# A weight slice loaded in two pieces, and the first four products in another order

## The chip, the cores and the metric

The kernel runs on one core of a Trainium2 chip. The metric is the device time of one execution in microseconds (us). Three executions of the kernel before took 1918.41, 1918.44 and 1919.22 us; the median is 1918.44.

## The reference, cut to what matters

One layer of a decoder trunk is computed for 320 tokens (256 of a prompt, 64 new ones of eight sequences), 2048 channels wide, in float32. All weights are read once.

```python
h = rmsnorm(x, norm_mix_g)
b_a, c_a, v_a, glu_a, glu_b, gate_a, gate_b = split(h @ w_in)        # 2048 -> 7 x 2048
y_a = (b_a * causal_dwconv3(c_a * v_a)) @ w_out_a
u = glu_a * sigmoid(glu_b)
z = silu(layernorm(causal_dwconv31(u) + bias))
y_b = z @ w_out_b
x = x + (sigmoid(gate_a) * y_a + sigmoid(gate_b) * y_b) @ w_o
h2 = rmsnorm(x, norm_ffn_g)
x = x + (silu(h2 @ w_gate) * (h2 @ w_up)) @ w_down                   # 2048 -> 5632 -> 2048
y = rmsnorm(x, final_norm_g)
```

The last rows of both convolutions' inputs are outputs as well.

## The kernel before, in words

**Products.** Every matrix product is made of 128 x 128 blocks of weights against 320 tokens. To keep float32's precision, weights and activations are each split in a high part (rounded to float32r) and a low part (the rest). Each block then needs three matmuls: weight high x activation high (line 268), weight high x activation low (line 270), weight low x activation high (line 272). In the code, `prod` in `begin` issues them, and its argument `which` selects one of the three (0, 1, 2).

**Units and pieces.** A unit is 256 output columns (two blocks j = 0 and 1, each with its own accumulator) over all of the contraction. Its weights come in pieces of four contraction chunks k, 512 KB each. ACT makes the high part and DVE the low part (lines 226 and 230 for whole pieces).

**The opening.** The first three units of `w_in` run as a group (`run_group`), because the activations also have to arrive. In the first round (r = 0, chunks k = 0 to 3) every chunk serves all three units m = 0, 1, 2 in turn. The weights of this round and the chunks of x are packed into few transfers: `op0` (the gains and x's chunk 0, into the tile `lead`), `op1` (chunk 0 of the three units' weights, 256 columns each) and `op2` (for k = 1 to 3: x's chunk and the three weight slices), all of these into the tile `opening`.

**Queues of the opening (lines 97 to 105).** SP issues `lead`; ACT issues the first 128 columns of unit 0's slice (64 KB); SP issues unit 0's second 128 columns with unit 1's 256 columns as one transfer (192 KB, line 99); ACT issues unit 2's slice (128 KB); SP goes on with the four transfers of `op2` (288, 256, 544 and 544 KB, line 104), and then, in `load_x` (line 117) and `load_part` (line 183), with further chunks of x and raw weight pieces. Later transfers are issued as earlier ones land.

**The splits of the opening.** `at_start` calls `x_chunk(k)`: x times its gain, high part (DVE, line 410, for k = 0 and 1; ACT, line 412, after that) and low part (DVE, line 413). Then `open_split(m, k)` for m = 0, 1, 2: high part on ACT (line 1032), low part on DVE (line 1033). For the very first slice the high part is made in two halves of 128 columns, the first from ACT's transfer and the second from SP's; its low part is one instruction over both halves. `in_turn` keeps the order on ACT and DVE.

**What sets the order.** A planner with a modelled time line orders the instructions of each engine, but `tc.issue_after(x)` holds an instruction behind x. In `run_group` the variable `last_mm` chains the matmuls: for k = 0 every product is chained to the one before it, so that they run exactly in the order of `turns`; for later k only every second product (j = 1) moves the chain on, and the planner may order the six matmuls of a pair. In `turns` an entry is (m, j, f): unit, block, and which of the three products (None for all).

Ahead of the first product TensorE runs 12 matmuls on zeros (line 123), which need no load.

Of the kernel before, what the change touches and what calls it, by code (L numbers as in the profile page):

```python
# [15 lines left out]
P = 128  # L16
# [14 lines left out]
NB = 256  # L31
# [8 lines left out]
def trunk_kernel(ctx: ExitStack, tc: tile.TileContext, a):  # L40
# [44 lines left out]
    sp, aq = nc.sync, nc.scalar  # L85
# [6 lines left out]
    opening = io.tile([P, 2 * D], F32, tag="pair", name="opening")  # L92
# [3 lines left out]
        opened[m][0] = opening[:, m * NB : (m + 1) * NB]  # L96
    sp.dma_start(out=lead, in_=a["op0"])
    aq.dma_start(out=opening[:, 0:P], in_=a["op1"][:, 0:P])
    sp.dma_start(out=opening[:, P : 2 * NB], in_=a["op1"][:, P : 2 * NB])
    warmed = aq.dma_start(out=opened[2][0], in_=a["op1"][:, 2 * NB :]).ins  # L100
    for k in range(1, KP):
        o = opening[:, 3 * NB + (k - 1) * W : 3 * NB + k * W]
# [85 lines left out]
    def load_to(i):  # L188
        while nload[0] <= min(i, len(pieces) - 1):
            load_part(nload[0], 0, pieces[nload[0]]["n"], sp)  # L190
            if nload[0] in after_load:
                after_load[nload[0]]()
            nload[0] += 1

    def split_to(i):
        while nsplit[0] <= min(i, len(pieces) - 1):
            q = pieces[nsplit[0]]
            if nsplit[0] > 2:
                load_to(nsplit[0])
            n = q["n"]  # L200
            if "apart" in q:
                q["hi"] = [slot("wh", F32R)[:, :NB] for _ in range(n)]
                q["lo"] = [slot("wl", F32R)[:, :NB] for _ in range(n)]
                for k in range(n):
                    last_split["ac"] = ac.copy(out=q["hi"][k], in_=q["raw"][:, k, :]).ins
                    last_split["ve"] = ve.tensor_tensor(
                        out=q["lo"][k], in0=q["raw"][:, k, :], in1=q["hi"][k].bitcast(F32), op=ALU.subtract
                    ).ins
                nsplit[0] += 1
                continue  # L210
            h = wp.tile([P, KP, NB], F32R, tag="whi", name=nm("whi"))
            l = wp.tile([P, KP, NB], F32R, tag="wlo", name=nm("wlo"))
            q["hi"], q["lo"] = h, l
            if nsplit[0] > 3:
                split(q, 0, n)
            nsplit[0] += 1
# [39 lines left out]
    def begin(u):  # L256
        acc = [ps_acc.tile([P, 512], F32, tag="acc", name=nm("acc")) for _ in range(u["nj"])]
        hi, lo = u["acts"]()
        hi_, lo_ = lambda k: alt(hi[k]), lambda k: alt(lo[k])
        nk = u["nk"]  # L260

        def prod(q, k, j, which=None):
            kk = q["ka"] + k
            wh = q["hi"][:, k, j * P : (j + 1) * P]
            wl = q["lo"][:, k, j * P : (j + 1) * P]
            o = acc[j][:, :T]
            if which in (None, 0):
                last = te.matmul(o, wh, hi_(kk), start=(kk == 0), stop=False)  # L268
            if which in (None, 1):
                last = te.matmul(o, wh, lo_(kk), start=False, stop=False)  # L270
            if which in (None, 2):
                last = te.matmul(o, wl, hi_(kk), start=False, stop=(kk == nk - 1))  # L272
            return last.ins

        return acc, prod
# [3 lines left out]
    def run_group(us, at):  # L279

        on = [begin(u) for u in us]
        for k in range(KP):
            u0 = [pieces[u["pieces"][0]] for u in us]
            if k == 0:
                turns = [(0, j, f) for j in range(2) for f in range(2)]
                turns += [(m, j, f) for f in range(2) for m in (1, 2) for j in range(2)]
                turns += [(m, j, 2) for m in range(3) for j in range(2)]
                for m in range(3):
                    at(0, m, k)
            else:  # L290
                turns = [(m, j, None) for m in range(3) for j in range(2)]
            for m, j, f in turns:
                if k and j == 0:
                    at(0, m, k)
                with tc.issue_after(last_mm[0]):
                    last = on[m][1](u0[m], k, j, f)
                if k == 0 or j:
                    last_mm[0] = last
        for r, m, k in [(r, m, k) for r in range(1, NC // KP) for m in range(3) for k in range(KP)]:
            u = us[m]  # L300
            pi = u["pieces"][r]
            acc, prod = on[m]
            load_to(pi + DMA_AHEAD)
            at(r, m, k)
            if k == 0:
                with tc.issue_after(x_last["ac"]), tc.issue_after(x_last["ve"]):
                    split_to(pi + 1)
            with tc.issue_after(last_mm[0]):
                for j in range(2):
                    last = prod(pieces[pi], k, j)  # L310
            last_mm[0] = last
            if r == NC // KP - 1 and k == KP - 1:
                u["post"](acc)
# [825 lines left out]
    load_to(6)  # L1139
    split_to(2)  # L1140
    run_group(first_units, at_start)
    for what, budget, kw in seq:
        if callable(what):
# [101 lines left out]
```

## Time and profile before

| what | value |
|---|---|
| median of three runs | 1918.44 us |
| the profiled execution's own time | 1918.46 us |
| its span, first to last instruction | 1916.3 us |
| TensorE (PE) busy | 1910.5 us, 14,071 matmuls |
| VectorE (DVE) busy | 1303.9 us |
| ScalarE (ACT) busy | 840.7 us |
| bytes moved by DMA | 321.18 MB |
| first product that belongs to the result | starts at 3.95 us |

How to read the profile: a row of the time line gives the start and the length in us, the engine, the line of the code, the operation, the tile written and the tile read, the shape, the count of merged instructions, and in brackets the idle time of that engine just before and what ended it. PE is the matrix engine and PEld its weight load. SPq and ACTq are issues of transfers by SP and ACT. In lists of transfers the last column is the time from issue to landing. Busy times of PE use modelled ends, so that a start is firmer than an end.

### The profile page before, as it was taken

Reading aid. Unit: us, or ns where it says so; the run is one execution under the profiler, and the core shown is the slowest. Engines: PE = TensorE matmul, PEld = TensorE weight load, DVE = VectorE, ACT = ScalarE, POOL = GpSimd, SP = SyncE. Lnnn points to the kernel's source line nnn. Section 1 sums busy time; section 2 is a strip of 40 time slices with the busy share of each in tenths; the row PEclk is TensorE's granted clock in tenths of the full one; section 3 lists DMA queues with packets and bytes.
Section 4 is the critical chain, followed back from the end, with each engine's and each line's share of the span. In section 5 each row is a group of like instructions: output and inputs, shape, how many; then the busy total and the mean of one; then the engine's idle time right before and its main releaser. Section 6 shows DMA issues by size and latency. Waiting matters only on the chain.

```text
span 1916.3 us, 33970 instructions
## 1 busy us (share of the span) xinstructions
PE 1910.5 (100%) x14071; PEld 1909.6 (100%) x14071; DVE 1303.9 (68%) x1951; ACT 840.7 (44%) x1203; POOL 5.0 (0%) x26
## 2 busy tenths in 40 slices
PE   9999999999999999999999999999999999999998
PEld 9999999999999999999999999999999999999998
DVE  8998888999898788546566655555444555555556
ACT  6544344444444346434445333433333433434543
POOL 0000000000000000000000000000000000000000
PEclk9999999999999999999999999999999999999999
DMA  8565655555555555555565555555555555554554
GB/s 294 177 183 161 196 157 167 161 165 159 165 164 163 159 163 165 159 162 165 164 188 188 163 158 164 164 158 157 160 167 164 165 162 159 164 163 147 176 158 131
DMA packets 96755, 321.18 MB, mean 168 GB/s; under 512 B 12792, under 2 KB 19512, under 8 KB 96568
## 3 DMA queue, kind: packets, MB, share of 16 engines
q1 hardware_dynamic: 96168, 318.61, 53.4%
q8 instruction: 110, 1.80, 0.4%
q10 hardware_dynamic: 432, 0.39, 0.1%
q14 instruction: 45, 0.37, 0.1%
HBM read 315.42 MB, written 4.98 MB: 167 GB/s over the span
## 4 chain that ended last, share of the span: by engine, by line
PE 99%; DMA 0%; DVE 0%; ACT 0%; issue 0%; DVEq 0%
PE acc L270 33%; PE acc L272 33%; PE acc L268 33%; PE acc L825 0%; PE acc L827 0%; PE acc L826 0%; DMA lead<-in_op 0%; PE acc L858 0%; PE acc L850 0%; DVE rl L413 0%; ACT junk L932 0%; DVE rh L410 0%; DVE ye L928 0%; DVE yo L928 0%; DVE rst L928 0%
## 5 line engine op out<-in xcount | busy, mean ns | idle before, releaser
L230 DVE TENSOR_TENSOR wlo<-raw,whi 128x1024 fp32r<-128x1024 f32 (+1 forms) x588 | 709.6, 1207 | 518.5 <-ACT whi L226 515.3
L226 ACT CAST whi<-raw 128x1024 fp32r<-128x1024 f32 (+1 forms) x588 | 607.0, 1033 | 948.5 <-PE acc L270 771.9
L270 PE MATMUL acc<-hl,whi 128*128 128x320 f32 x1600 | 478.1, 299 | 0.0
L272 PE MATMUL acc<-hh,wlo 128*128 128x320 f32 x1600 | 478.0, 299 | 0.0
L268 PE MATMUL acc<-hh,whi 128*128 128x320 f32 x1600 | 477.8, 299 | 0.0
L268 PE MATMUL acc<-gh,whi 128*128 128x320 f32 x1408 | 421.0, 299 | 0.0
L270 PE MATMUL acc<-gl,whi 128*128 128x320 f32 x1408 | 421.0, 299 | 0.0
L272 PE MATMUL acc<-gh,wlo 128*128 128x320 f32 x1408 | 421.0, 299 | 0.0
L270 PEld LDWEIGHTS acc<-hl,whi 128*128 128x128 f32 x1600 | 302.3, 189 | 0.0
L272 PEld LDWEIGHTS acc<-hh,wlo 128*128 128x128 f32 x1600 | 302.3, 189 | 0.0
L268 PEld LDWEIGHTS acc<-hh,whi 128*128 128x128 f32 x1600 | 302.2, 189 | 0.0
L490 DVE SCALAR_TENSOR_TENSOR cb<-win,prm,cb 128x320 f32<-128x320 f32 x480 | 262.4, 549 | 9.3
L268 PEld LDWEIGHTS acc<-gh,whi 128*128 128x128 f32 x1408 | 266.1, 189 | 0.0
L270 PEld LDWEIGHTS acc<-gl,whi 128*128 128x128 f32 x1408 | 266.1, 189 | 0.0
L272 PEld LDWEIGHTS acc<-gh,wlo 128*128 128x128 f32 x1408 | 266.1, 189 | 0.0
L270 PE MATMUL acc<-fl,whi 128*128 128x320 f32 x672 | 200.9, 299 | 0.0
L268 PE MATMUL acc<-fh,whi 128*128 128x320 f32 x672 | 200.8, 299 | 0.0
L272 PE MATMUL acc<-fh,wlo 128*128 128x320 f32 x672 | 200.8, 299 | 0.0
L268 PEld LDWEIGHTS acc<-fh,whi 128*128 128x128 f32 x672 | 127.0, 189 | 0.0
L270 PEld LDWEIGHTS acc<-fl,whi 128*128 128x128 f32 x672 | 127.0, 189 | 0.0
L272 PEld LDWEIGHTS acc<-fh,wlo 128*128 128x128 f32 x672 | 127.0, 189 | 0.0
L268 PE MATMUL acc<-ah,whi 128*128 128x320 f32 x256 | 76.5, 299 | 0.0
(198 smaller groups left out, 2068.0 us busy)
## 6 DMA issues: line engine op xcount, KB each, us to landing
raw<-in_w_in SPq DMA_DIRECT2D x221, 512.0 KB, 3.7
raw<-in_w_gate SPq DMA_DIRECT2D x88, 512.0 KB, 3.6
raw<-in_w_up SPq DMA_DIRECT2D x88, 512.0 KB, 3.6
raw<-in_w_down SPq DMA_DIRECT2D x80, 512.0 KB, 3.7
raw<-in_w_out_a SPq DMA_DIRECT2D x32, 512.0 KB, 3.6
raw<-in_w_out_b SPq DMA_DIRECT2D x32, 512.0 KB, 3.6
raw<-in_w_o SPq DMA_DIRECT2D x32, 512.0 KB, 3.7
raw<-in_w_down SPq DMA_DIRECT2D x16, 256.0 KB, 2.7
```

The lines of the kernel that those rows point to most:

```text
L226: return ac.copy(out=q["hi"][:, ks, :], in_=q["raw"][:, ks, :]).ins
L230: return ve.tensor_tensor(out=q["lo"][:, ks, :], in0=q["raw"][:, ks, :], in1=q["hi"][:, ks, :].bitcast(F32), op=ALU.subtract).ins
L268: last = te.matmul(o, wh, hi_(kk), start=(kk == 0), stop=False)
L270: last = te.matmul(o, wh, lo_(kk), start=False, stop=False)
L272: last = te.matmul(o, wl, hi_(kk), start=False, stop=(kk == nk - 1))
L490: ve.scalar_tensor_tensor(out=o, in0=win[0][:, :, j + 2 : j + 10], scalar=w_cb(j, c), in1=o, op0=ALU.mult, op1=ALU.add)
```

## The change

The transfer of line 99 becomes two, both on SP and in this order: columns 128 to 255 (the second half of unit 0's slice, 64 KB), then columns 256 to 511 (unit 1's slice, 128 KB). The four transfers of `op2` and all that SP issues after them come behind one more issue. And in `turns` the four products of unit 0's first chunk that use the weights' high part are taken with the product index outermost: both blocks by x's high part, then both by x's low part. Before, block 0 had both of its products ahead of block 1's.

```diff
     sp.dma_start(out=lead, in_=a["op0"])
     aq.dma_start(out=opening[:, 0:P], in_=a["op1"][:, 0:P])
-    sp.dma_start(out=opening[:, P : 2 * NB], in_=a["op1"][:, P : 2 * NB])
+    for w0, w1 in ((P, NB), (NB, 2 * NB)):
+        sp.dma_start(out=opening[:, w0:w1], in_=a["op1"][:, w0:w1])
     warmed = aq.dma_start(out=opened[2][0], in_=a["op1"][:, 2 * NB :]).ins
...
             if k == 0:
-                turns = [(0, j, f) for j in range(2) for f in range(2)]
+                turns = [(0, j, f) for f in range(2) for j in range(2)]
                 turns += [(m, j, f) for f in range(2) for m in (1, 2) for j in range(2)]
                 turns += [(m, j, 2) for m in range(3) for j in range(2)]
```

## The prediction

> **What bounds the kernel now.** I read the page's first line, busy times and chain first, then a table of stretches, and last the opening 11 us in order of time.
>
> ```profile
> span 1916.3 us, 33970 instructions
> PE 1910.5 (100%) x14071; PEld 1909.6 (100%) x14071; DVE 1303.9 (68%) x1951; ACT 840.7 (44%) x1203; POOL 5.0 (0%) x26
> ...
> PE 99%; DMA 0%; DVE 0%; ACT 0%; issue 0%; DVEq 0%
> ```
>
> ```profile
> 3.90:5.07 1.17, 1.08 (x6) 0.74 (x5) 0.89 (x3) 0.72 (x3) 0.00 (x0) 1.00 1.04 314
> 5.07:9.49 4.42, 4.42 (x34) 4.41 (x33) 3.24 (x10) 2.41 (x8) 0.00 (x0) 1.00 1.01 375
> 9.49:10.17 0.68, 0.68 (x6) 0.49 (x4) 0.68 (x4) 0.68 (x4) 0.00 (x0) 1.00 1.09 423
> 10.17:1900.00 1889.83, 1889.83 (x13921) 1889.83 (x13921) 1287.11 (x1890) 830.25 (x1174) 3.52 (x17) 1.00 0.54 167
> ```
>
> In the second fence the columns are the stretch, its length, and busy time with count for PE, PEld, DVE, ACT and POOL, then clock, DMA share and GB/s. From 10.17 us to 1900 us TensorE runs 13,921 matmuls in 1889.83 us, 0.1358 us each, the clock full and PE busy without a break. A change in the opening can therefore do one thing to the end: move the moment at which this unbroken run begins. The DMA share is about 1 from 3.9 us on, so the opening is fed at the rate of the DMA engines. Busy PE hides short waits, because a matmul counts until its modelled end; I look for starts that are further apart than 0.136 us.
>
> ```profile
> 3.95 0.40 PE L268 MATMUL acc<-rh,whi 128*128 128x320 f32 x1
> 4.45 0.40 PE L270 MATMUL acc<-rl,whi 128*128 128x320 f32 x1
> 4.70 0.40 PE L268 MATMUL acc<-rh,whi 128*128 128x320 f32 x1
> 4.94 0.30 PE L270 MATMUL acc<-rl,whi 128*128 128x320 f32 x1
> 5.07 0.78 PE L268 MATMUL acc<-rh,whi 128*128 128x320 f32 x4
> ...
> 9.36 0.30 PE L272 MATMUL acc<-rh,wlo 128*128 128x320 f32 x1
> 9.49 0.30 PE L268 MATMUL acc<-rh,whi 128*128 128x320 f32 x1
> 9.63 0.37 PE L270 MATMUL acc<-rl,whi 128*128 128x320 f32 x1
> 9.93 0.40 PE L272 MATMUL acc<-rh,wlo 128*128 128x320 f32 x1
> 10.17 0.30 PE L268 MATMUL acc<-rh,whi 128*128 128x320 f32 x1
> ```
>
> There are two loose places. The first is the start, where the four products of the first slice begin at 3.95, 4.45, 4.70 and 4.94. The second is k = 2: from 9.36 to 10.17 four steps take 0.81 us instead of 4 x 0.136 = 0.54, so **0.27 us** is waited there. Between them 4.42 us hold 34 starts, 0.13 us each: no wait. What releases the second place:
>
> ```profile
> 8.39 0.56 ACT L412 ACTIVATE rh<-opening,lead 128x320 fp32r<-128x320 f32 x1 [0.71 <-DMA opening<-in_op]
> ...
> 8.99 0.55 DVE L413 SCALAR_TENSOR_TENSOR rl<-opening,lead,rh 128x320 fp32r<-128x320 f32 x1 [0.83 <-ACT rh L412]
> 9.46 0.75 DVE L1033 TENSOR_TENSOR wlo<-opening,whi 128x256 fp32r<-128x256 f32 x2
> ```
>
> ACT stands idle 0.71 us for the third chunk's transfer, then x's high half (8.39), its low half (8.99) and the weight's low half (9.46, some 0.42 long) follow each other, and the matmul at 9.93 takes the last. PE waits for a chain that starts at a landing. Whatever is won before 9.4 us is waited away here, unless that landing moves too.
>
> **The change, part by part.** It has two parts: one more transfer on SP, and a new order for the first four products. No arithmetic is added or removed; PE keeps its 14,071 matmuls.
>
> ```profile
> 1.19 0.42 SPq L99 DMA_DIRECT2D opening<-in_op  x1
> 1.65 1.85 SPq L104 DMA_DIRECT2D opening<-in_op  x4
> ...
> 8.32 0.33 SPq L183 DMA_DIRECT2D raw<-in_w_in  x1
> ```
>
> ```profile
> lead<-in_op SPq DMA_DIRECT2D x1, 168.0 KB, 2.7
> opening<-in_op ACTq DMA_DIRECT2D x1, 64.0 KB, 2.8
> opening<-in_op SPq DMA_DIRECT2D x1, 288.0 KB, 4.2
> opening<-in_op SPq DMA_DIRECT2D x1, 256.0 KB, 4.8
> opening<-in_op SPq DMA_DIRECT2D x1, 544.0 KB, 5.7
> opening<-in_op SPq DMA_DIRECT2D x1, 544.0 KB, 6.6
> ```
>
> *SP's queue.* One issue lasts 0.46 us (1.65 - 1.19). The second unit's slice is now issued at 1.65, the four transfers of the later chunks at 2.11 and on, and the loads behind them (activations, the first raw weights) up to as much later. Does the k = 2 landing move by 0.46? The four are issued 1.85 / 4 = 0.46 us apart, but take 4.2, 4.8, 5.7 and 6.6 us to land: each stands 0.6 to 0.9 us longer than the one ahead. They wait in the queue for bytes ahead of them, and those bytes are the same. The third was issued at 1.65 + 2 x 0.46 = 2.57 and landed at about 8.3; the lead, with almost nothing ahead, needed 2.7 for 168 KB. At the 375 GB/s of the second stretch the further 376 KB cost 1.0 us, so 3.7 would be needed, and 5.7 - 3.7 = 2.0 us of its time is queueing. The later issue is hidden by that: I take 0, with 0.46 as the case that the queue runs dry. Later loads are issued as earlier ones land (the one at 8.32 right behind the landing at 8.3), so they follow the landings and not the added slot.
>
> *The added packets.* Where 128 rows of 1.5 KB went, 128 of 0.5 KB and 128 of 1 KB go.
>
> ```profile
> q1 hardware_dynamic: 434, 0.68, 46.7%
> q10 hardware_dynamic: 288, 0.20, 13.4%
> ```
>
> These are packets, MB and share of 16 engines up to 4.6 us. q10, which carries ACT's two transfers of just those row sizes, used 0.134 x 16 x 4.6 = 9.9 us of engine time: 34 ns a packet, 49 us a MB. q1, with rows of 1.3 KB and more, used 34.4 us, 51 us a MB. Small rows cost no more per byte, which puts the low bound at 0. The high bound lets each of 128 + 16 added packets cost a whole average packet: 144 x 34 ns / 16 engines = 0.31 us. I take 0.05 us, near the low end, since the two rates agree. A gain is excluded: ACT waits for this landing, and the bytes ahead of it do not shrink.
>
> [...]
>
> *The first four products.* They are now half 0 x high, half 1 x high, half 0 x low, half 1 x low.
>
> ```profile
> 4.35 0.30 ACT L1032 CAST whi<-opening 128x128 fp32r<-128x128 f32 x1 [0.45 <-DMA opening<-in_op]
> 4.55 0.71 ACT L1032 CAST whi<-opening 128x256 fp32r<-128x256 f32 x2
> ...
> 3.84 0.55 DVE L413 SCALAR_TENSOR_TENSOR rl<-lead,rh 128x320 fp32r<-128x320 f32 x1
> ```
>
> Now half 1's cast starts at 4.35 and its matmul at 4.70, 0.35 later. The 64 KB transfer lands at 1.19 + 2.8 = 3.99 if it goes like ACT's 64 KB, and at 4.35 if it gains nothing from its size. The second product then comes at 4.35 to 4.70, the fourth two to three steps later; x's low half, ready at 4.39, is no longer waited for when half 1 is late. If half 1 gains nothing, the wait to 4.70 has lost its cover, the low product that ran at 4.45, and the fourth product comes 0.14 us later. The second unit's cast, now at 4.55, must wait for a transfer issued 0.46 later: from 4.35 (same bytes, queue full) to 4.81 (all the delay felt). Its first matmul follows a cast's start by 0.52 (4.55 to 5.07), so at 4.87 to 5.33: **-0.20 to +0.26 us** against 5.07. The third unit's cast is next on ACT and moves with it, as do the products by w's low half.
>
> *What hides this.* k = 1 is next, and there a stream that comes sooner or later meets these:
>
> ```profile
> 6.32 0.55 DVE L413 SCALAR_TENSOR_TENSOR rl<-opening,lead,rh 128x320 fp32r<-128x320 f32 x1
> 6.79 0.42 DVE L1033 TENSOR_TENSOR wlo<-opening,whi 128x256 fp32r<-128x256 f32 x1
> ...
> 7.32 0.43 PE L270 MATMUL acc<-rl,whi 128*128 128x320 f32 x2
> 7.59 0.43 PE L272 MATMUL acc<-rh,wlo 128*128 128x320 f32 x2
> ```
>
> x's low half is ready at 6.87 and used at 7.32, w's at 7.21 and used at 7.59, so 0.2 us sooner fits. At k = 2 the wait of 0.27 becomes 0.47 in the one case and 0.01 in the other, and the matmul at 9.93 stays where its operand puts it. If the cover were gone, 0.26 would come through.
>
> **Sum.** Products 0, slot 0, packets +0.05: the unbroken run begins at 10.22 instead of 10.17. The profiled execution took 1918.46 us for its span of 1916.3, 2.16 around it, and stands 0.02 over the median of 1918.44. 1918.46 + 0.05 = **1918.5 us**, the span 1916.35.
>
> **The rivals.** (1) *Slower: the slot counts.* At SP's queue the four opening transfers move by the whole 0.46 us and k = 2 with them: 1918.9. It decides once 2.0 us of queueing is used up, or if the engines pause between the two new pieces. For it: the landing is what PE waits for. Against it: the landings are 1.1 to 1.4 us apart for issues 0.46 apart.
>
> (2) *Faster: the planner regroups k = 2.* Only pairs of products are chained there, so inside a pair it is free. At k = 2 it puts low weights third; at k = 1 (rows above: two L270, then two L272) they come fifth, 0.27 later. With that order the wait between 9.63 and 9.93 (0.30 less 0.136, 0.16 us) and some of the 0.10 behind it (10.17 - 9.93 less 0.136) would go, about 0.2 in all: 1918.3. For it: new times in the planner's model. Against: nothing in the diff touches that pair.
>
> (3) *The change does not do what it says.* The 64 KB interleaves with ACT's second transfer and lands no earlier than 4.3; the fourth product loses 0.14, k = 2 swallows it: 1918.5 as well.
>
> (4) *The plan shifts far behind.* The order of ACT's and DVE's work comes from modelled times, and a late pair of splits costs PE its length.
>
> ```profile
> L230 DVE TENSOR_TENSOR wlo<-raw,whi 128x1024 fp32r<-128x1024 f32 (+1 forms) x588 | 709.6, 1207 | 518.5 <-ACT whi L226 515.3
> L226 ACT CAST whi<-raw 128x1024 fp32r<-128x1024 f32 (+1 forms) x588 | 607.0, 1033 | 948.5 <-PE acc L270 771.9
> ```
>
> 1.03 + 1.21 = 2.24 us a time; two such places make 1922.9. Against it: 13,921 matmuls without a break.
>
> **How the numbers follow.** Forecast 0.66, (1) 0.13, (2) 0.12, (3) 0.06, (4) 0.03. About 0.2% of the time, 3.8 us, is what a measurement can tell from no change. Only (4) reaches that: slower 0.02, and 0.01 for faster from a cause that I do not see; within it 0.97. The range takes in (2) and (1), 1918.3 to 1918.9, the packets' high bound (1918.8), and the scatter of the three runs shown, 0.8 us from lowest to highest: 1917.9 to 1919.4.
>
> **What would show it.** Right: half 1's cast before 4.35; the first matmul of the second unit within 4.87 to 5.33; the wait at k = 2 grown or shrunk by the same amount; PE from about 10.2 on with 0.1358 us a matmul. The third chunk's landing near 8.35 says packets, near 8.8 says rival 1. Low weights fifth at k = 2 says rival 2. A break in PE after 11 us, or more than 1 us of change, would make the prediction wrong.

## The result

The changed kernel takes **1921.54 us** (median of 22 runs, 1919.48 to 1924.03), the kernel before 1918.68 (22 runs, 1918.20 to 1919.37): +2.86 us, a ratio of 1.0014 with a 95% interval of 1.0008 to 1.0020. The forecast was 1918.5. No run of the one lies within the runs of the other. The profiled execution is one of the quicker ones, 1920.35 us for a span of 1918.2, so its trace shows +1.9 us and not all of the loss. The page and its chain:

```profile
span 1918.2 us, 33972 instructions
...
PE 1910.7 (100%) x14071; PEld 1910.0 (100%) x14071; DVE 1303.5 (68%) x1951; ACT 840.6 (44%) x1203; POOL 5.0 (0%) x26
...
PE 99%; DMA 0%; DVE 0%; ACT 0%; SPq 0%; issue 0%; DVEq 0%
```

Work and busy time are those of before; the chain now has a share of SP's issues in it. PE's opening in order of time (lines are one higher than before):

```profile
4.10 0.82 PE L269 MATMUL acc<-rh,whi 128*128 128x320 f32 x2
4.72 0.68 PE L271 MATMUL acc<-rl,whi 128*128 128x320 f32 x2
7.09 0.84 PE L269 MATMUL acc<-rh,whi 128*128 128x320 f32 x4 [1.69 <-ACT whi L1033]
7.77 0.71 PE L271 MATMUL acc<-rl,whi 128*128 128x320 f32 x4
...
11.57 0.30 PE L269 MATMUL acc<-rh,whi 128*128 128x320 f32 x1
11.71 0.30 PE L271 MATMUL acc<-rl,whi 128*128 128x320 f32 x1
11.84 0.30 PE L273 MATMUL acc<-rh,wlo 128*128 128x320 f32 x1
11.98 0.30 PE L269 MATMUL acc<-rh,whi 128*128 128x320 f32 x1
```

The four products of unit 0 run as the change wants them. Then PE stands idle until the second unit's first product at **7.09**, 2.02 us later than before (5.07). From 7.77 on it runs without a break, at k = 2 too, which now begins at 11.57 and has its starts 0.14 apart. The 0.27 us that PE waited there before are gone, and 0.06 us are added by short waits among the four products at 7.09 (0.68 us to 7.77; before, 0.62 from 5.07 to 5.69): 2.02 - 0.27 + 0.06 = 1.81 of the 1.9 us of span. The product that stood at 10.17 now stands at 11.98, 1.81 later as well. What the idle stretch waits for, on ACT and in the list of transfers (last column: us from issue to landing):

```profile
3.67 0.50 ACT L1033 CAST whi<-opening 128x128 fp32r<-128x128 f32 x2 [0.51 <-DMA opening<-in_op]
6.63 1.12 ACT L1033 CAST whi<-opening 128x256 fp32r<-128x256 f32 x3 [2.46 <-DMA opening<-in_op]
```

```profile
opening<-in_op SPq DMA_DIRECT2D x1, 64.0 KB, 2.7
opening<-in_op SPq DMA_DIRECT2D x1, 128.0 KB, 5.0
opening<-in_op SPq DMA_DIRECT2D x1, 288.0 KB, 5.2
```

The second half of unit 0 lands in 2.7 us, at 3.89 (both of its casts are over at 3.67 + 0.50 = 4.17, before at 4.65), but unit 1's 128 KB, issued at 1.65, take 5.0. Meanwhile the DMA engines move little. The table of stretches from 3.3 to 4.8 us, before and after (last columns: PEclk, DMA share, GB/s):

```profile
3.30:4.80 1.50, 1.41 (x7) 0.98 (x6) 1.06 (x3) 0.75 (x3) 0.00 (x0) 1.00 1.08 346
```

```profile
3.30:4.80 1.50, 1.50 (x7) 1.39 (x7) 1.27 (x3) 0.50 (x2) 0.00 (x0) 1.00 0.71 106
```

The rate falls from 346 to 106 GB/s, but the busy share of the engines only from 1.08 to 0.71. So they are not simply out of work: 0.71 x 16 engines x 1.5 us for 0.16 MB (106 GB/s in 1.5 us) is some 107 us of engine time a MB, where before it was 1.08 x 16 x 1.5 for 0.52 MB, 50 us a MB. Two questions follow: what makes the slice land late, and where the rest of the median's 2.86 us is.

### The profile page after: what moved, and what is told of

Same layout as the page of the kernel before. It is cut to its first block, busy times and chain, and to the rows that moved or that the text cites. A ratio compares the mean times of both kernels' runs of the same rounds, so it can differ in the third digit from the quotient of the medians.

```text
span 1918.2 us, 33972 instructions
## 1 busy us (share of the span) xinstructions
PE 1910.7 (100%) x14071; PEld 1910.0 (100%) x14071; DVE 1303.5 (68%) x1951; ACT 840.6 (44%) x1203; POOL 5.0 (0%) x26
## 4 chain that ended last, share of the span: by engine, by line
PE 99%; DMA 0%; DVE 0%; ACT 0%; SPq 0%; issue 0%; DVEq 0%
PE acc L269 33%; PE acc L273 33%; PE acc L271 33%; DMA opening<-in_op 0%; PE acc L828 0%; PE acc L827 0%; PE acc L826 0%; PE acc L859 0%; PE acc L851 0%; ACT junk L933 0%; SPq L100 0%; ACT whi L1033 0%; SPq L97 0%; DVE ye L929 0%; DVE yo L929 0%
```

## The experiments

All are compared with runs of the kernel before on the same chip. (e14 and e15 are one more profiled execution each of the changed kernel and of the kernel before, and are not in the table.) The interval of a ratio is about +-0.0009 (1.7 us), so by itself it tells few of them from no change; where I go further, I go by how the single runs lie.

| kernel | median, us (runs) | before | ratio [95%] | GB/s, 3.3 to 4.8 us |
|---|---|---|---|---|
| e1_split_only | 1919.87 (1919.48-1921.53) | 1918.86 | 1.0008 [0.9999, 1.0017] | 148 |
| e2_order_only | 1918.85 (1918.46-1919.36) | 1918.86 | 1.0000 [0.9991, 1.0009] | 300 |
| e3_row_halves | 1921.16 (1919.54-1921.78) | 1918.86 | 1.0010 [1.0001, 1.0019] | 203 |
| e4_slice_on_act | 1920.47 (1919.88-1922.30) | 1918.86 | 1.0010 [1.0002, 1.0019] | 189 |
| e5_tiny_ahead | 1920.11 (1919.64-1922.24) | 1918.77 | 1.0010 [1.0001, 1.0019] | 160 |
| e6_tiny_behind | 1919.30 (1918.70-1920.40) | 1918.77 | 1.0003 [0.9994, 1.0012] | 337 |
| e7_slices_in_one | 1918.85 (1918.23-1919.34) | 1918.77 | 1.0001 [0.9992, 1.0009] | 330 |
| e8_split_behind | 1918.97 (1918.40-1919.38) | 1918.77 | 1.0001 [0.9992, 1.0010] | 343 |
| e9_filler | 1920.02 (1919.73-1920.77) | 1918.65 | 1.0007 [0.9997, 1.0016] | 169 |
| e10_two_on_act | 1918.99 (1918.51-1921.36) | 1918.65 | 1.0001 [0.9993, 1.0010] | 290 |
| e11_slice_with_k1 | 1921.70 (1919.64-1923.55) | 1918.65 | 1.0014 [1.0005, 1.0023] | 176 |
| e12_bridge | 1920.74 (1919.05-1921.86) | 1918.65 | 1.0009 [1.0000, 1.0018] | 342 |
| e13_slice_on_pool | 1919.52 (1919.06-1921.10) | 1918.76 | 1.0005 [0.9996, 1.0014] | 176 |

### Which part of the change

e1 splits the transfer and keeps the old order of products; e2 takes the new order and keeps the transfer whole.

```diff
 # e1, against before
-    sp.dma_start(out=opening[:, P : 2 * NB], in_=a["op1"][:, P : 2 * NB])
+    for w0, w1 in ((P, NB), (NB, 2 * NB)):
+        sp.dma_start(out=opening[:, w0:w1], in_=a["op1"][:, w0:w1])
 # e2, against before
-                turns = [(0, j, f) for j in range(2) for f in range(2)]
+                turns = [(0, j, f) for f in range(2) for j in range(2)]
```

> Only the transfer is split; the four products keep the order of before. Theory A (the split makes the second unit's slice land late, whatever the order of the products): about +2 to +3 us, 1920.5 to 1921.7, with that slice landing near 6.6 us after the start and PE idle for about 2 us before its first product. Theory B (the new order loses the cover of the wait for the second half): within 0.3 us of before, slice landing near 4.4.

> Only the order of the four products is new; the 192 KB transfer stays whole. Theory A: within 0.3 us of before, since 0.14 us lost at the start is waited away at k = 2. Theory B: +2 us or more.

The order alone is free: +0.0. The split alone costs +1.0; its interval just takes in no change, but ten of its eleven runs lie above all 33 of the kernel before. The runs lie in two groups with nothing between, six from 1919.48 to 1919.87 and five from 1921.19 to 1921.53. In its profile the slice takes 4.1 us:

```profile
opening<-in_op SPq DMA_DIRECT2D x1, 128.0 KB, 4.1
```

That is less than in the changed kernel (5.0), and theory A had expected the full +2 to +3. Of the two parts the split is the one that costs. The landing varies (4.3 in e9, which loads as the change does), and a step of about 1.7 us lies on top of it. Whether the new order adds something to the loss once the transfer is split is not shown.

### Row sizes, queues, number of transfers

```diff
 # e3, against the change: halves by partitions, rows of 1.5 KB
-    for w0, w1 in ((P, NB), (NB, 2 * NB)):
-        sp.dma_start(out=opening[:, w0:w1], in_=a["op1"][:, w0:w1])
+    for r0, r1 in ((0, P // 2), (P // 2, P)):
+        sp.dma_start(out=opening[r0:r1, P : 2 * NB], in_=a["op1"][r0:r1, P : 2 * NB])
 # e4, against the change: unit 1's slice on ACT, ahead of unit 2's
+    sp.dma_start(out=opening[:, P:NB], in_=a["op1"][:, P:NB])
+    aq.dma_start(out=opening[:, NB : 2 * NB], in_=a["op1"][:, NB : 2 * NB])
 # e5, against before: 8 KB that nobody reads, ahead of the 192 KB (e6: behind them)
+    tiny = const.tile([P, 16], F32, name="tiny")
+    sp.dma_start(out=tiny, in_=a["op1"][:, 0:16])
     sp.dma_start(out=opening[:, P : 2 * NB], in_=a["op1"][:, P : 2 * NB])
```

> The change, but the 192 KB are split by partitions (two transfers of 64 rows of 1.5 KB) instead of by columns: one more transfer on SP as in the change, the packets of before. Theory A1 (one more transfer in SP's row of opening transfers is what costs): again +2 us or more, landings late. Theory A2 (the short rows of 0.5 and 1 KB cost): within 0.4 us of before.

> The change, but the second unit's slice (128 KB, rows of 1 KB) is issued by ACT ahead of the third unit's slice, so that SP issues as many transfers as before. Theory A1: within 0.4 us of before. Theory A2: +2 us or more, as the rows are as short as in the change.

> The kernel before with one added transfer that nobody reads (128 rows of 64 bytes, 8 KB) on SP ahead of the 192 KB transfer. Theory C (the number of opening transfers counts, not their bytes: an added one drains the engines' queues after 3.3 us): +0.8 to +3 us, the DMA rate between 3.5 and 4.5 us falls below 200 GB/s. Theory D (what counts is only that the second unit's slice stands in a transfer of its own issued at 1.65 or later): here the slice is also issued at 1.65, so the same. If within 0.3 us of before, the slot by itself is harmless and the small transfers of the change are at fault.

> The same added transfer of 8 KB, but behind the 192 KB one. Theory C: the DMA rate falls as in the change between 3.5 and 5 us, and the chunk k = 1 lands late, so +0.5 to +2 us. Theory D: the slice is issued at 1.19 as before and lands near 4.3, so within 0.3 us of before.

e3 has the row size of before and loses 2.3 us: the short rows are not the cause (A2 falls). e4 issues as many transfers on SP as the kernel before and loses 1.6. There unit 1's slice is ACT's second issue; the third unit's slice, now ACT's third, is late, and ACT waits 2.39 us for it:

```profile
6.99 1.42 ACT L1033 CAST whi<-opening 128x256 fp32r<-128x256 f32 x4 [2.39 <-DMA opening<-in_op]
```

So SP's queue is not special (A1 falls as far as it means SP). e5 moves only 8 KB more, but puts the unchanged 192 KB in third place on SP: +1.3, with no run below 1919.64. e6 adds the same 8 KB one place later: +0.5, which the interval does not tell from no change, and the rate stays at 337 GB/s. That is more than theory D's 0.3 and without theory C's fall of the rate. Bytes and packets are equal in e5 and e6; the place of the slices is what differs.

```diff
 # e7, against before: one transfer of 320 KB in place of 192 KB on SP and 128 KB on ACT
+    sp.dma_start(out=opening[:, P : 3 * NB], in_=a["op1"][:, P : 3 * NB])
 # e8, against before: the 256 KB of chunk 1 in two
-        for w0, w1 in ((0, T + NB), (T + NB, W)) if k == 1 else ((0, W),):
+        for w0, w1 in ((0, T + NB), (T + NB, T + 2 * NB), (T + 2 * NB, W)) if k == 1 else ((0, W),):
```

> The kernel before with one transfer less: the 192 KB and ACT's 128 KB become one of 320 KB on SP. Theory C: the rate stays above 300 GB/s up to 5 us; the products of the second unit start later, as 320 KB land near 4.6, but k = 2 absorbs that: 0 to -0.3 us against before. Theory D: no prediction beyond +-0.3 us.

> The kernel before with the 256 KB transfer of chunk 1 split in two of 128 KB: as many transfers as the change, but the split stands behind the first-chunk slices and the first 288 KB. Theory C: the rate falls somewhere between 3.5 and 6 us and k = 1 or k = 2 waits, +0.5 us or more. Theory D: within 0.3 us of before, since the slice is issued at 1.19 and enough bytes are queued by the time of the split.

Neither can be told from before. e8 has as many opening transfers as the change, so the number alone (theory C) does not do it.

### The step of 1.7 us: PE's clock

```diff
 # e9, against the change: 12 matmuls on zeros between unit 0's four products and unit 1's
+                if (k, m, j, f) == (0, 1, 0, 0):
+                    for _ in range(12):
+                        with tc.issue_after(last_mm[0]):
+                            last_mm[0] = te.matmul(spin[:, :T], ...).ins
```

> The change with 12 matmuls on zeros added between the first four products and the second unit's, where PE stands idle for about 2 us; they change no output. Theory E (the transfers cost about 1 us to 2 us, and in half of the runs a further 1.7 us come from PE's clock falling to half for one window because PE stood idle): the group of runs at 1921.2 and more disappears, all runs lie within 1 us of 1920.2. Theory F (the whole scatter comes from the landings): median and scatter as in the change, 1919.5 to 1924.

> The changed kernel once more, one look. Theory S: the slice lands between 5.7 and 7 us again, and SP's fourth transfer (288 KB) only 0.5 to 1.2 us behind it. If the slice lands below 5 us in this look, the late landing of the first look was an accident.

e14 is the changed kernel itself, executed and profiled once more: 1921.93 us, 1.58 more than its first profile. The slice takes the same 5.0 us and PE resumes at the same 7.09. The difference lies behind it. Busy PE with the number of matmuls from 6.96 to 10.37, first profile and then e14:

```profile
6.96:10.37 3.41, 3.28 (x24) 3.28 (x25) 2.94 (x8) 2.42 (x8) 0.00 (x0) 1.00 1.01 405
```

```profile
6.96:10.37 3.41, 3.28 (x12) 3.28 (x13) 2.94 (x8) 2.42 (x8) 0.00 (x0) 1.00 1.02 406
```

PE does 12 matmuls where it did 24; 12 x 0.136 = 1.63 us. In e14 the first products behind the gap start 0.3 us apart (1.23 us for four, 0.68 in the first profile):

```profile
7.09 1.43 PE L269 MATMUL acc<-rh,whi 128*128 128x320 f32 x4 [1.60 <-ACT whi L1033]
8.32 1.01 PE L271 MATMUL acc<-rl,whi 128*128 128x320 f32 x3
```

The clock column shows nothing of this, because it reads 1.00 until the first record of the clock in a trace. That record gives full rate from 5.21 us in the first profile; in e14 the 12 matmuls from 6.96 to 10.37 are followed by 27 from 10.37 to 13.78. Both executions begin at half rate: the matmuls on zeros start 0.27 us apart, twice 0.136 (the last at 3.57 and 3.84 in the first profile; in e14 two in 0.54, from 3.57 to 4.11). So in e14 the clock did not fall in the gap. It had not risen yet, and it stayed at half behind the gap, up to 10.37. The stretches ahead of the rise, and behind it in the first profile (first two rows: first profile, last row: e14):

```profile
1.79:5.21 3.42, 3.42 (x14) 3.15 (x12) 1.45 (x6) 1.86 (x4) 0.29 (x2) 1.00 0.82 194
5.21:8.62 3.41, 1.72 (x12) 1.53 (x12) 1.52 (x4) 1.72 (x5) 0.00 (x0) 1.00 0.99 378
```

```profile
3.55:6.96 3.41, 1.94 (x7) 1.40 (x6) 1.19 (x3) 0.82 (x4) 0.00 (x0) 1.00 0.86 292
```

In the first profile PE was busy for all of the 3.42 us ahead of the rise; in e14 it was busy for 1.94 us of the 3.41 up to 6.96, and no rise followed there. In two profiles the clock fell after it had risen, e11 (its edit is shown further down) and then e4:

```profile
3.70:7.11 3.41, 1.28 (x7) 0.80 (x5) 0.99 (x3) 0.60 (x3) 0.00 (x0) 1.00 0.92 309
7.11:10.52 3.41, 3.07 (x11) 3.07 (x12) 3.05 (x9) 2.97 (x10) 0.00 (x0) 0.50 1.02 404
```

```profile
3.97:7.39 3.42, 1.44 (x8) 0.94 (x6) 1.22 (x3) 1.03 (x5) 0.00 (x0) 1.00 0.98 325
7.39:10.80 3.41, 3.36 (x12) 3.36 (x13) 3.18 (x9) 2.51 (x8) 0.00 (x0) 0.50 0.98 384
```

After a window in which PE was busy 1.28 us of 3.41 (e4: 1.44 of 3.42), the clock is 0.50 for a window of 3.41 us, with 11 matmuls (12). It had risen before, for a matmul ahead of the fall took 0.18 us of busy time in both (1.28 / 7, 1.44 / 8), against 0.28 at half rate in e14 (1.94 / 7). After 1.72 us of 3.41, in the first profile of the change, it stayed full. The windows ahead of the two falls were not idle, and PE's idle stretch in e11 was 2.47 us:

```profile
7.45 0.63 PE L269 MATMUL acc<-rh,whi 128*128 128x320 f32 x1 [2.47 <-ACT whi L1033]
```

In the two profiles of the change PE's idle stretch was much the same, 1.69 and 1.60 us, and the clock rose at 5.21 in the one and at 10.37 in the other. When it changes, then, decides whether a run pays; what sets the moment is not shown. Four profiles caught it, all of runs at 1920.94 us or more: in e4, e11 and e14 PE does 12, 11 and 12 matmuls in the 3.41 us of the rows above, and in e13 the first four products behind the gap take 1.23 us (6.31 to 7.54), as in e14. In the profiles of the change and of e9, at 1920.44 us or less, the rate behind the gap is full: 24 matmuls from 6.96 to 10.37 in the one, four products in 0.54 us (7.30 to 7.84) in the other.

e9 keeps PE busy in the gap, and the upper group is gone: 11 runs from 1919.73 to 1920.77, where the change had 1919.48 to 1924.03. Theory E holds. Its median is 1.37 over before, without overlap (before: up to 1919.46), against 2.86 for the change. But this is not the price of the late slice alone, for the fillers hold up PE:

```profile
5.20 2.27 PE L300 MATMUL spin<-const-float32-0.0 128*128 128x320 f32 x12
7.30 0.71 PE L270 MATMUL acc<-rh,whi 128*128 128x320 f32 x4
```

In this profile unit 1's slice landed at about 5.95 (1.65 + 4.3), and its product, which follows the landing by 0.48 in the change (1.65 + 4.96 = 6.61 to 7.09), could have come at some 6.4 instead of 7.30 (an estimate). The change's own 22 runs give the price without fillers. Nine lie from 1919.48 to 1920.70, with a median of 1920.19, 1.51 over before, and thirteen from 1921.45 to 1924.03: **about 1.5 us are the late slice, and the clock adds about 1.4 us to the median**. The two slowest runs (1923.35 and 1924.03) lie 2.65 and 3.33 us above the slowest of the nine, more than one window at half rate cost in e14 (1.63); no profile caught such a run, and this stays open.

### Bytes queued, or the place in the queue

```diff
 # e10, against the change: unit 1's and unit 2's slices in one transfer on ACT
+    sp.dma_start(out=opening[:, P:NB], in_=a["op1"][:, P:NB])
+    warmed = aq.dma_start(out=opening[:, NB : 3 * NB], in_=a["op1"][:, NB : 3 * NB]).ins
 # e11, against the change: unit 1's slice packed with the first part of chunk 1, 416 KB
+    sp.dma_start(out=opening[:, P:NB], in_=a["op1"][:, P:NB])
+    warmed = aq.dma_start(out=opened[2][0], in_=a["op1"][:, NB : 2 * NB]).ins
+    sp.dma_start(out=opening[:, 2 * NB : 4 * NB + T], in_=a["op3"])
 # e12, against the change: 256 KB that nobody reads behind unit 2's slice in ACT's transfer
+    third = const.tile([P, 3 * NB], F32, name="third")
+    opened[2][0] = third[:, 0:NB]
+    warmed = aq.dma_start(out=third, in_=a["op4"]).ins
 # e13, against the change: unit 1's slice issued by POOL
+    sp.dma_start(out=opening[:, P:NB], in_=a["op1"][:, P:NB])
+    nc.gpsimd.dma_start(out=opening[:, NB : 2 * NB], in_=a["op1"][:, NB : 2 * NB])
```

> Unit 0's second half alone on SP (64 KB) as in the change, but units 1 and 2 in one transfer of 256 KB on ACT: eight opening transfers as before, and as many bytes issued by the second issue of each queue as before (528 KB with the lead less nothing). Theory G (engines that run out of queued bytes near 3.3 us stop and need more than 1 us to get going again): no fall of the DMA rate below 200 GB/s, time within 0.4 us of before. Theory H (a short second transfer on SP by itself delays what follows): again +1 us or more.

> Unit 0's second half alone on SP, and unit 1's slice packed with the first part of chunk 1 as one transfer (416 KB): eight opening transfers as before, but only 424 KB issued by the second issue of each queue. Theory G: the rate falls below 200 GB/s after 3.3 us and the time is +1 us or more, though the number of transfers is that of before. Theory C (number of transfers): within 0.4 us of before apart from the later landing of the second unit's slice, at most +1 us.

> The change as it is, nine transfers, but ACT's second transfer carries 256 KB more, which nobody reads. Theory G: with these bytes queued the engines do not run dry, the rate stays above 250 GB/s, and the time comes back to within 0.7 us of before although 0.7 us of more bytes are moved. Theory C: +1.5 us or more, as in the change or worse.

> The change, but the second unit's slice is issued by POOL, as the first transfer of a third queue. Theory S (a transfer that is issued third on its queue, at about 1.65 us, lands near 6 us whatever its size; the slice must be issued first or second on a queue): the slice lands before 5 us, the time is within 0.5 us of before. Theory G (the engines run out of queued bytes near 3.3 us): 424 KB are queued by the second issues of SP and ACT and 128 KB by POOL, 552 KB as before, so also within 0.5 us. If it is +1 us or more, both fall.

> The kernel before once more, one look. Theory S: SP's third transfer (288 KB) lands at 5.4 to 6.5 us, as before (1.65 + 4.2), though it is more than twice the slice; the DMA rate from 3.3 to 4.8 us stays above 290 GB/s.

e10 brings the time back (+0.3, not told from before, with one run of eleven at 1921.36) and has the short second transfer on SP, so theory H falls. e11 has the number of transfers of before and loses 3.05: C falls for good. Theory G had said both. Theory S fits them too, but it was only put down after e9 to e12, so for these it forecast nothing. e12 speaks against G. With 256 KB more queued the rate is that of before, 342 GB/s, and yet the slice takes 4.5 us and the median is 2.1 over before, not 0.7:

```profile
3.30:4.80 1.50, 1.39 (x5) 0.90 (x4) 0.87 (x2) 0.45 (x2) 0.00 (x0) 1.00 1.00 342
```

```profile
opening<-in_op SPq DMA_DIRECT2D x1, 128.0 KB, 4.5
```

So the slice was late while the engines were busy. This is not clean, since the added 256 KB are some 0.7 us of the 4.5 (at 375 GB/s), and the runs of e12 split too: five from 1919.05 to 1919.84, about as G had said, and six from 1920.74 to 1921.86; its profile, 1921.62, is of the upper group. e12 leans to S and does not settle it. What the slow kernels other than e13 share is that a slice needed early stands third on its queue. Issued third on SP, at 1.65 us (e3: 1.81), the time to landing was:

| KB | us to landing, one profile each |
|---|---|
| 8 | 3.1 (e6) |
| 96 | 4.2 (e3) |
| 128 | 4.1 (e1), 4.3 (e9), 4.5 (e12), 5.0 (change), 5.0 (e14) |
| 192 | 4.3 (e5) |
| 288 | 3.7 (e8), 4.2 (before), 4.5 (e15), 4.5 (e7), 4.5 (e10), 4.7 (e13), 4.8 (e2), 5.1 (e4) |
| 416 | 5.3 (e11) |

From 96 to 288 KB the size tells nothing. But the rows also differ in what stands ahead: 552 KB (168 and 192 on SP, 64 and 128 on ACT) for the 288 KB of the kernel before, 424 KB (168, 64, 64 and 128) for the 128 KB of the change and for the 288 KB of e4, the slowest of its row. So the table does not part the place from the bytes ahead, and fewer bytes ahead did not bring an earlier landing. e15, the kernel before once more (1918.75 us), kept its rate at 290 GB/s. Transfers in second place took 2.6 to 3.4 us for 8 to 256 KB: 2.6 for the 8 KB of e5, 2.7 for the 64 KB of the change and 3.4 for those of e12, 3.2 for the 192 KB of e6, and in e10 3.3 for 256 KB:

```profile
opening<-in_op ACTq DMA_DIRECT2D x1, 256.0 KB, 3.3
```

In the kernel before the third place held chunk 1, which is needed only at 7; the change put the second unit's slice there, needed at 5. e13 is between the theories. POOL's first transfer was issued at 1.24 and took as long as a third one:

```profile
opening<-in_op POOLq DMA_DIRECT2D x1, 128.0 KB, 4.6
```

The time came down to +0.76 us, not to the 0.5 that both theories had named, and the rate fell to 176 GB/s though 552 KB had been issued by then. So neither "third on its queue" nor the bytes queued is the whole rule. Nor did the engines stop, as G had it: in all kernels with a rate of 106 to 203 GB/s their share was 0.59 to 0.89, which is 61 to 107 us of engine time a MB against 47 to 56 in the others, worked out as above. Why a transfer that starts at this moment of the opening lands so late is **open**: the runs show that it does, not what inside the DMA does it.

e10 also shows what the change's idea brought when the slice was not delayed. PE at k = 2:

```profile
9.37 0.30 PE L272 MATMUL acc<-rh,wlo 128*128 128x320 f32 x1
9.86 0.40 PE L268 MATMUL acc<-rh,whi 128*128 128x320 f32 x1 [0.19 <-ACT whi L1032]
10.15 0.40 PE L270 MATMUL acc<-rl,whi 128*128 128x320 f32 x1
10.48 0.40 PE L272 MATMUL acc<-rh,wlo 128*128 128x320 f32 x1
10.72 0.30 PE L268 MATMUL acc<-rh,whi 128*128 128x320 f32 x1
```

The second product of unit 0's slice by x's high part starts at 4.63 in this profile, 0.07 us sooner than before, but at 9.37 nothing is left of it (before: 9.36). PE then waits at k = 2 again, 1.35 us for four steps (before: 0.81; without a wait 0.54), so a gain ahead of it would have been waited away. No version tried beats the kernel before.

## Why the prediction was wrong

**What bounds the kernel: right.** After the opening PE ran without a break as before, and the whole result lies in when this run begins.

**The order of the first products: right.** Worth 0.0 alone (e2). The second half did land sooner, at 3.89, just ahead of the 3.99 to 4.35 that were given, and the four products were done before unit 1's slice was there.

**The second unit's slice: wrong, the step that failed.** The cast was put at 4.35 (same bytes, queue full) to 4.81 (all the delay felt), so PE at 4.87 to 5.33. It was 6.63 and 7.09. The time of a landing was taken from its bytes and from the transfer it was cut from, which stood in second place. The nearest row was another: SP's transfer in third place, 288 KB, 4.2 us, which stood in the prediction's own fence. All four of SP's later landings, this 4.2 among them, had been read as waiting for the bytes ahead (for one of 544 KB it was worked out: "5.7 - 3.7 = 2.0 us of its time is queueing"), and from that the later issue was called hidden, the term "slot 0" of the sum. With that row the slice's upper bound would have been 1.65 + 4.2 = 5.85, PE 1.3 us later at the first product and about 1.0 us at the end. The third chunk was not hidden from it either: ACT's wait for that landing ended at 9.45 (before 8.39), where the prediction had named 8.35 or 8.8 for the landing. PE came there later still and did not wait for it.

**What hides it: right as a mechanism, too small.** The wait at k = 2 was swallowed to the last, 0.27 us of 2.02.

**Rival 1: its sign was right, its price was not.** It named the queue and "if the engines pause between the two new pieces", but priced a pause with one issue, 0.46 us, and looked for it at k = 2. The late slice cost about 1.5, at unit 1's first product.

**The clock: not in the prediction.** It adds about 1.4 us to the median. That PE's clock would stay at half behind a wait of 1.60 us (e14), or fall to half for 3.41 us in one of 2.47 (e11), was no rival and had no price.

**The packets: not what cost.** e3, with rows of the size of before, still lost 2.3 us. The 0.05 us of the sum is too small for these runs to tell. **Rivals 2 and 4 (the planner): did not happen.** ACT and DVE run the same instructions in the same order, and PE's pair at k = 2 still has the low weights third (11.57, 11.71, 11.84 above). **Rival 3** did not happen; the half landed sooner.

**What a measurement can tell: put too high.** The prediction had 3.8 us. With 22 runs of each kernel the interval of the loss is 1.5 to 3.8 us, well clear of zero.

## What to carry to other kernels

In an opening like this one, price a transfer by the row that stands in its place in the order of issue, not by a row of its size: from second place to third the time to landing went from 2.6 to 3.4 us up to 3.7 to 5.3 here, and the size did not tell it. Where a change makes PE wait as long as here, add the clock: behind waits of 1.60 us (e14) and 2.47 us (e11) PE ran at half rate for up to 3.41 us, behind one of 1.69 us (first profile) it did not. In the times it showed first as two groups. And a small transfer that is split off for an early start should not push back one that is needed soon after.

## What was not expected of the hardware

Transfers issued third on SP, at about 1.65 us, landed 3.7 to 5.3 us later for anything from 96 to 416 KB. An 8 KB transfer that nobody reads cost 1.3 us ahead of the slices (e5) and 0.5 behind them (e6). While the slice was late, the DMA engines were busy for 0.71 of the time at less than a third of the rate. The same program, with the slice landing at the same time, differed by 1.58 us through PE's clock alone (first profile and e14).
